# Loading the mixed weight block through GpSimd's DMA queue, and three planned landing times, in a tanh-gated product of matrices on Trainium2

## The chip, the cores and the metric

The kernel runs on one core of a Trainium2 chip. A core has a matrix engine (TensorE, PE in the profile, with its weight loads shown apart as PEld), three engines for elementwise work (VectorE or DVE, ScalarE or ACT, GpSimd or POOL), a queue engine that only issues transfers (SyncE or SP) and 16 DMA engines that move data between HBM and the core's memories. The metric is the device time of one launch in microseconds; lower is better.

## The reference

```python
def setup_inputs():
    batch, m, k, n = 16, 512, 1024, 768
    ...
def reference(x, w1, w2):
    y1 = np.matmul(x, w1)
    y2 = np.matmul(x, w2)
    return (np.tanh(y1) * y2).astype(np.float32)
```

x is 16 x 512 x 1024, w1 and w2 are 1024 x 768, all float32. Read as one matrix, x has 8192 rows, which are 64 row tiles of 128. Each output row tile is 128 x 768.

## The kernel before

**Blocks.** The kernel works in float16 with float32 sums. The two weight matrices are kept in one tile `wh`, cut into three column blocks of 512: block a is the first 512 columns of w1, block b the first 512 of w2, and block g (the mixed block) the last 256 columns of w1 beside the last 256 of w2. Along the contraction each block has eight slices of 128 rows, k = 0 to 7, in two halves of four (`KH` = 4). A slice of a block is named by both: a5 is slice 5 of block a; the two parts of a slice of g come from w1 (t = 0) and from w2 (t = 1).

**Head.** The first four row tiles (`HEAD` = 4) are multiplied plainly: for each row tile, each block and each slice, one matrix instruction of 512 columns (L420). This work is what TensorE does while the weights come in: block a first, then g, then b. The rows of these tiles are transposed on TensorE (L370), and so are those of row tiles 4, 5 and 6; the transposed rows are copied out of PSUM by ScalarE or VectorE (L356, L358).

**Triples.** The other 60 row tiles are worked in 20 triples. Three row tiles with two halves of the contraction and three column blocks would be 18 products of half a contraction each; a scheme with sums of operands does with 15 (`C_OPS`, names p0 to p14). Each product is four matrix instructions of 512 columns (L443). Its operands are blocks of x or sums of them, named by a bit mask: x1 and x2 are the two halves of a triple's first row tile, x4 and x8 of its second, x16 and x32 of its third. VectorE makes the ten sums of x for each triple (L411, for instance x3 = x1 + x2, x11 = x3 - x8, x15 = x11 - x4) and, once, the eleven sums of weight blocks (L402). ScalarE copies some results out of PSUM (L447), VectorE adds them up (L453), ScalarE takes the tanh (L456) and VectorE multiplies (L461). The order of the products is a fixed list; the first triple begins with p7 (x16 with a weight block), p10 (x32), p1 (x3), p6 (x15), p12, p9.

**The order of everything else** comes from a planner in the file (`Planner`). Each operation has a cost on each engine that may do it, a due time, and what it needs. The planner runs a simulated clock with these costs and writes out every engine's instructions in the order of its simulated starts. An engine then works through its list in that order on the chip: when an instruction at the head waits, all those behind it wait. How well the written order fits therefore depends on the planner's guesses, above all on when transfers land. Two kinds of guess are touched here:

- For the first loads there is a table `lands`. From a clock of 9.2 us on, each load in turn adds its size (`size`: 0.68 for half a row tile or a slice of a, 0.75 for a part of g, 0.63 for a slice of b, 1.25 for a row tile), and what would land after 21.5 us gets 1.2 us on top (`LAG_FROM`, `LAG`).
- A DMA transpose of a later row tile (operation T, issued by SP at L377) is planned to land its `latency` after its turn on the planner's one transfer line: 1.0 us for row tiles 7 to 9, and 3.0 us from row tile 10 on.

**Loads of the weights.** Slices a0 to a3 go out from ScalarE's queue and a4 to a7 from SP's (L347), as float32 into a staging area (`arena`), from which VectorE casts them into `wh` (L358). Block g follows on SP's queue in eight loads (L344); one load brings slices k and k + 4 of one of the two matrices, 128 partitions times two runs of 256 float32 numbers. When both matrices' parts have landed, slices k and k + 4 are cast into `wh`: slice 0 by VectorE (L358), the seven others by ScalarE (L356). Block b is loaded by GpSimd's queue in eight loads of one slice (L349), whose transfer itself turns float32 into float16, so that nothing is staged or cast. GpSimd is held back by a small instruction that reads a slice of `wh` (`gate`, L483): it begins its loads when slice g0 is cast. Behind block b on the same queue come the row tiles 6, 4 and 5 in this order (`rows_in`, L352, with the cast in the transfer too), and then all later row tiles. From row tile 10 on, each of these loads stands behind a second small instruction (`hold_loads`, L480) that waits for the transpose of the row tile four before.

Beside this, ScalarE sums the absolute values of every row tile and every weight slice (L380); at the end a flag is made of the sums, and only if they lie outside a range does a slower general path run.

Of the kernel before, what the change touches and what calls it, by code (L numbers as in the profile page):

```python
# [226 lines left out]
def kernel(  # L227
# [7 lines left out]
    nc = tc.nc  # L235
# [3 lines left out]
    KO = K // P  # L239
    KH = KO // 2  # L240
# [71 lines left out]
    def wf(s, k, n=1):  # L312
        j = slices.index((s, k)) % SLOTS
        return arena[:, j * F:(j + n) * F]
# [27 lines left out]
    def load_w(e, s, k, t=None):  # L342
        if s == "g":
            pin(nc.sync.dma_start(wf(s, k, 2).rearrange("p (h t n) -> p h t n", h=2, t=2)[:, :, t, :],  # L344
                                  wr[t].rearrange("p (h q) n -> p h q n", h=2)[:, :, k, F:]))
        elif s == "a":
            pin((nc.scalar if k < 4 else nc.sync).dma_start(wf(s, k), wr[0][:, k, :F]))  # L347
        else:
            pin(nc.gpsimd.dma_start(w_cols(s, k), wr[1][:, k, :F]))  # L349
# [170 lines left out]
    for n, what in enumerate(on_sp):  # L520
        before = [f"L{on_sp[n - 1]}"] if n else []
        if what[0] == "x":
            op(f"L{what}", {"sp": 0.05}, 0.1 * n - 100, [], load_first, int(what[1]), int(what[2]), issued=before, lands=lands[what])
        else:
            s, k = what[0], int(what[1])
            j = slices.index((s, k))
            old = [slices[i - SLOTS] for i in range(j, j + 1 + (s == "g")) if i >= SLOTS]
            op(f"L{what}", {"sp": 0.05}, 0.1 * n - 100, [], load_w, s, k, int(what[2]) if s == "g" else None, issued=before,
               behind=[f"c{a}{b}" for a, b in old], lands=lands[what])
    op("gate", {"pool": 0.1}, 0.0, ["c%s%d" % GATE], gate, *GATE)  # L530
    for n, what in enumerate(late):
        op(f"c{what}", {"pool": 0.58}, 0.1 * n, [], load_w, "b", int(what[1]), issued=[f"c{late[n - 1]}" if n else "gate"], lands=lands[what])
    for n, mt in enumerate(rows_in):
        op(f"L{mt}", {"pool": 0.58}, 1 + 0.1 * n, [], load_x, mt, issued=[f"L{rows_in[n - 1]}" if n else f"c{late[-1]}"],
           behind=[f"cx{m}{h}" for m in range(2, HEAD) for h in range(2) if xh_place(m) == xh_place(mt)], lands=lands[f"x{mt}"])

    landed = {}
    for s, k in slices:
        loads = [f"g{k % KH}{t}" for t in range(2)] if s == "g" else [f"{s}{k}"]
        landed[s, k] = max(lands[n] for n in loads)  # L540
        if s != "b":
            op(f"c{s}{k}", CAST.get(f"{s}{k}", CAST[s]), landed[s, k] + 0.3, [f"L{n}" for n in loads], cast_w, s, k)
    all_casts = [f"c{s}{k}" for s, k in slices if s != "b"]
    for t in range(2):
        for k in range(KO):
            late = START + 32 + 8 * (t * KO + k)
            op(f"aw{t}{k}", {"act": 0.81}, late + 6, [f"cg{k}", f"c{'ab'[t]}{k}"], abs_w, t, k, hold=late)

# [23 lines left out]
    def plain(mt, s, due, behind=()):  # L572
        for n, k in enumerate([k for u, k in slices if u == s]):
            before = list(behind) + ([f"m{mt}{s}0"] if n else [])
            op(f"m{mt}{s}{k}", {"pe": MM}, due(n), [f"c{s}{k}", f"e{mt}{k // KH}"], mm, (s, mt), mt, k, w_cols(s, k), n == 0,
               behind=before, chains=[(s, mt)])
        last = [f"m{mt}{s}{k}" for k in range(KO)]
        xt_readers[mt] += last
        return last
# [60 lines left out]
    def w_needs(v, ks=slice(0, KH)):  # L640
        if v in wsum:
            return [f"B{v}.{p.start}" for p in parts(v) if p.start < ks.stop and ks.start < p.stop]
        bit = v.bit_length() - 1
        return [f"c{s}{bit // 3 * KH + k}" for s in "abg"[bit % 3] for k in range(ks.start, ks.stop)]

# [81 lines left out]
    for mt in range(BY_PE, MT):  # L727
# [3 lines left out]
        if mt >= BY_PE + FREE:  # L731
# [133 lines left out]
```

## Time and profile before

| | |
|---|---|
| median of 3 runs | 298.4 us (298.35 to 298.59) |
| the profiled execution | 298.26 us, of which the profile's span is 296.7 us |
| TensorE busy | 289.9 us, 98% of the span, 1374 instructions |
| VectorE busy | 257.4 us, 87% |
| ScalarE busy | 225.9 us, 76% |
| GpSimd busy | 49.9 us, 17% |
| granted clock of TensorE | 0.999 |

TensorE is busy nearly all the time, so a microsecond can be won or lost only where it starts late, waits, or ends late. A busy share doesn't say whether its instructions follow each other at full pace, since the ends of matrix instructions are modelled; the distance from one start to the next does. A row of the timeline gives the start, the time taken, engine, line, operation, tiles written and read, and how many instructions are merged into it; in brackets stands the idle time ahead of it and what ended it. `arena` is the staging area for weights in the head and a buffer for partial results later; `early_x` is the first rows' buffer and later that of the sums of x.

### The profile page before, as it was taken

What the parts mean: (1) busy time and instruction counts of PE and PEld (TensorE: products, weight loads), DVE (VectorE), ACT (ScalarE), POOL (GpSimd) and SP (SyncE); (2) the same over time, 40 slices, a digit from 0 to 9 for tenths busy, and PEclk for the clock granted to TensorE, in tenths of its full rate; (3) what the DMA queues carried; (4) which work ended last, traced back from release to release, by engine and by line L of the source; (5) the groups of instructions that cost most, each with busy time, mean ns of one, the idle gap of its engine ahead of it and who ended that gap; (6) DMA issues with size and microseconds to landing.
All of it is one profiled execution on the core that took longest, in us unless ns stands there. A gap on an engine that the chain in (4) does not pass through costs nothing. (4 is left out here: it accounts for less than half of the span.)

```text
span 296.7 us, 4680 instructions
## 1 busy us (share of the span) xinstructions
PE 289.9 (98%) x1374; PEld 132.3 (45%) x1374; DVE 257.4 (87%) x552; ACT 225.9 (76%) x453; POOL 49.9 (17%) x129
## 2 busy tenths in 40 slices
PE   7999999999999999999999999999999999999994
PEld 3444444444444444444444444444444444444442
DVE  1679899989999998888989898898989989898784
ACT  2686898799978979797797988768687776868441
POOL 0073034032210321102111021111121100000000
PEclk9999999999999999999999999999999999999999
DMA  6999999999999999999999999999999999440334
GB/s 218 388 305 207 180 154 166 202 220 250 225 222 170 232 290 246 209 176 218 248 257 225 234 253 210 187 201 268 216 272 268 197 202 228 194 161 32 128 142 162
DMA packets 84427, 63.51 MB, mean 214 GB/s; under 512 B 62768, under 2 KB 66608, under 8 KB 84400
## 3 DMA queue, kind: packets, MB, share of 16 engines
q1 hardware_dynamic: 73600, 44.84, 63.2%
q0 software_dynamic: 9792, 16.78, 37.7%
q10 hardware_dynamic: 1008, 1.57, 1.5%
q8 instruction: 11, 0.18, 0.3%
q14 instruction: 16, 0.13, 0.1%
HBM read 39.85 MB, written 25.17 MB: 219 GB/s over the span
## 5 line engine op out<-in xcount | busy, mean ns | idle before, releaser
L443 PE MATMUL bank<-b,early_x 128*128 128x512 f16 x640 | 148.3, 379 | 0.1
L443 PEld LDWEIGHTS <-early_x 128*128 128x128 f16 x800 | 78.1, 98 | 95.0 <-issue 0.7
L453 DVE TENSOR_TENSOR bank<-bank,arena 128x512 f32<-128x512 f32 x100 | 69.7, 698 | 14.8 <-ACT arena L447 9.3
L447 ACT ACTIVATE arena<-bank 128x512 f32<-128x512 f32 x100 | 59.2, 596 | 28.4 <-PE bank L443 28.2
L461 DVE TENSOR_TENSOR o<-o,bank 128x256 f32<-128x256 f32 (+1 forms) x132 | 64.4, 513 | 6.1 <-ACT o L456 5.5
L380 ACT ACTIVATE junk<-xh 128x1024 f16<-128x1024 f16 x60 | 63.3, 1056 | 0.2
L443 PEld LDWEIGHTS <-xT 128*128 128x128 f16 x400 | 39.0, 98 | 47.2 <-issue 1.1
L443 PE MATMUL bank<-b,xT 128*128 128x512 f16 x240 | 58.3, 379 | 0.0
L456 ACT ACTIVATE o<-bank 128x256 f32<-128x256 f32 (+1 forms) x80 | 34.4, 436 | 16.8 <-DVE bank L453 12.9
L443 PE MATMUL bank<-wh,xT 128*128 128x512 f16 x160 | 41.1, 379 | 0.3 <-DVE bank L453 0.3
L443 PE MATMUL bank<-wh,early_x 128*128 128x512 f16 x160 | 40.9, 379 | 0.0
L480 POOL CAST held<-xT 128x1 f32<-128x1 f16 x54 | 13.0, 241 | 152.4 <-DMA xT<-xh 152.4
L352 POOL DMA_DIRECT2D xh<-in_x_dram x60 | 31.7, 529 | 23.3 <-ACT o L456 10.4
L411 DVE TENSOR_TENSOR early_x<-early_x,xT 128x512 f16<-128x512 f16 x80 | 33.3, 420 | 0.5
L447 ACT ACTIVATE bank<-bank 128x512 f32<-128x512 f32 x40 | 21.6, 575 | 7.6 <-DVE bank L453 6.4
L456 ACT ACTIVATE o<-arena 128x512 f32<-128x512 f32 x40 | 25.1, 628 | 1.3 <-DVE arena L453 1.1
L420 PE MATMUL bank<-wh,xT 128*128 128x512 f16 x72 | 18.6, 379 | 0.3 <-ACT xT L356 0.2
L411 DVE TENSOR_TENSOR early_x<-xT,xT 128x512 f16<-128x512 f16 x40 | 16.8, 421 | 0.0
L411 DVE TENSOR_TENSOR early_x<-xT,early_x 128x512 f16<-128x512 f16 x40 | 16.8, 420 | 0.0
L453 DVE TENSOR_TENSOR bank<-arena,bank 128x512 f32<-128x512 f32 x20 | 13.9, 695 | 2.3 <-ACT o L456 0.7
L453 DVE TENSOR_TENSOR arena<-bank,arena 128x512 f32<-128x512 f32 x20 | 13.7, 684 | 0.1
L453 DVE TENSOR_TENSOR arena<-arena,bank 128x512 f32<-128x512 f32 x20 | 13.6, 682 | 0.0
(47 smaller groups left out, 136.0 us busy)
## 6 DMA issues: line engine op xcount, KB each, us to landing
out_dram<-o SPq DMA_DIRECT2D x60, 384.0 KB, 5.6
xh<-in_x_dram POOLq DMA_DIRECT2D x60, 256.0 KB, 6.8
arena<-in_w_dram SPq DMA_DIRECT2D x12, 256.0 KB, 5.5
early_x<-in_x_dram SPq DMA_DIRECT2D x8, 256.0 KB, 5.0
arena<-in_w_dram ACTq DMA_DIRECT2D x4, 256.0 KB, 5.9
wh<-in_w_dram POOLq DMA_DIRECT2D x8, 128.0 KB, 5.4
xT<-xh SPq DMA_TRANSPOSE x57, 7.1
out_dram<-o SPq DMA_DIRECT2D x4, 128.0 KB, 2.2
```

The source lines that it names most:

```text
L352: pin(nc.gpsimd.dma_start(xh(mt), xf[mt]))
L380: pin(nc.scalar.activation(junk[:, :src.shape[-1]], src, ACT.Abs, scale=scale, accum_out=sums[:, column:column + 1]))
L411: pin(engine[e].tensor_tensor(x_operand(i, v), x_operand(i, a), x_operand(i, b), OP[how]))
L420: pin(nc.tensor.matmul(bank(chain)[:, :rhs.shape[-1]], xt(mt)[:, k, :], rhs, start=first, stop=k == KO - 1, skip_group_check=True))
L443: pin(nc.tensor.matmul(place(i, dst), x_operand(i, a)[:, k, :], w_rhs(b, k), start=begins and k == 0, stop=k == KH - 1, skip_group_check=T ...
L447: pin(nc.scalar.activation(place(i, dst), place(i, src), ACT.Copy, scale=float(sign)))
L453: pin(nc.vector.tensor_tensor(place(i, dst), a, b, ALU.add if signs == (1, 1) else ALU.subtract))
L456: pin(nc.scalar.activation(out_tile(HEAD + 3 * i + r)[:, lo:lo + n], place(i, src)[:, :n], ACT.Tanh, scale=float(sign)))
L461: pin(nc.vector.tensor_tensor(o, o, place(i, src)[:, at:at + n], ALU.mult))
L480: pin(nc.gpsimd.tensor_copy(held, xt(mt)[:, 0, :1]))
```

## The change

Three things are edited.

- Block g is no longer loaded by SP as float32 and cast afterwards. GpSimd's queue loads it with the cast in the transfer, straight into `wh`: eight loads as before, of slices k and k + 4 of one matrix, ahead of the eight loads of block b. The casts of g on VectorE (one) and ScalarE (seven) are gone, and so are the waits for their staging slots.
- GpSimd's gate waits for the cast of slice a5 in place of that of g0. In the table `lands`, a part of g adds 0.7 us in place of 0.75. A load of g has the same planned cost on GpSimd as one of b, 0.58 us.
- The planned latency of the transposes of row tiles 10, 11 and 12 becomes 5.8, 4.1 and 3.9 us in place of 3.0 (`LANDING`).

Since the planner runs anew with other numbers, the order of all engines' instructions may change with this, beyond the lines that are edited; the fixed order of the products doesn't.

```diff
+    LANDING = {HEAD + 6: 5.8, HEAD + 7: 4.1, HEAD + 8: 3.9}
...
         if s == "g":
-            pin(nc.sync.dma_start(wf(s, k, 2).rearrange("p (h t n) -> p h t n", h=2, t=2)[:, :, t, :],
-                                  wr[t].rearrange("p (h q) n -> p h q n", h=2)[:, :, k, F:]))
+            pin(nc.gpsimd.dma_start(wh[:, k::KH, F + t * G:F + t * G + G], wr[t][:, k::KH, F:]))
...
-    CAST = {"a": {"dve": 0.37}, "g": {"act": 0.495}, "g0": {"dve": 0.37}}
+    CAST = {"a": {"dve": 0.37}}
...
-    on_sp = "x00 x10 x20 x30 x01 x11 a4 a5 x21 a6 x31 a7".split() + [f"g{k}{t}" for k in range(KH) for t in range(2)]
-    late = [f"b{k}" for s, k in slices if s == "b"]
+    on_sp = "x00 x10 x20 x30 x01 x11 a4 a5 x21 a6 x31 a7".split()
+    late = [f"g{k}{t}" for k in range(KH) for t in range(2)] + [f"b{k}" for s, k in slices if s == "b"]
     rows_in = (HEAD + 2, HEAD, HEAD + 1)
-    GATE = ("g", 0)
+    GATE = ("a", 5)
     in_order = on_sp[4:] + late + [f"x{mt}" for mt in rows_in]
-    size = {"x": 0.68, "a": 0.68, "g": 0.75, "b": 0.63}
+    size = {"x": 0.68, "a": 0.68, "g": 0.7, "b": 0.63}
...
     for n, what in enumerate(late):
-        op(f"c{what}", {"pool": 0.58}, 0.1 * n, [], load_w, "b", int(what[1]), issued=[f"c{late[n - 1]}" if n else "gate"], lands=lands[what])
+        op(f"c{what}", {"pool": 0.58}, 0.1 * n, [], load_w, what[0], int(what[1]), int(what[2:] or 0), issued=[f"c{late[n - 1]}" if n else "gate"], lands=lands[what])
...
+    def cast(s, k):
+        return [f"cg{k % KH}{t}" for t in range(2)] if s == "g" else [f"c{s}{k}"]
...
-        loads = [f"g{k % KH}{t}" for t in range(2)] if s == "g" else [f"{s}{k}"]
-        landed[s, k] = max(lands[n] for n in loads)
-        if s != "b":
-            op(f"c{s}{k}", CAST.get(f"{s}{k}", CAST[s]), landed[s, k] + 0.3, [f"L{n}" for n in loads], cast_w, s, k)
+        landed[s, k] = max(lands[n[1:]] for n in cast(s, k))
+        if s == "a":
+            op(f"ca{k}", CAST["a"], landed[s, k] + 0.3, [f"La{k}"], cast_w, s, k)
...
-           behind=xt_readers[mt - XT_BUFS] if mt >= XT_BUFS and mt - XT_BUFS != HEAD - 1 else [], xfer=1.2, latency=1.0 if mt < HEAD + 6 else 3.0)
+           behind=xt_readers[mt - XT_BUFS] if mt >= XT_BUFS and mt - XT_BUFS != HEAD - 1 else [], xfer=1.2, latency=LANDING.get(mt, 1.0 if mt < HEAD + 6 else 3.0))
```

More of the change, by code (lines that the diff above doesn't have):

```diff
@@ L524 @@
         else:
[L525 to L529, printed above, removed]
+            op(f"L{what}", {"sp": 0.05}, 0.1 * n - 100, [], load_w, "a", int(what[1]), issued=before, lands=lands[what])
     op("gate", {"pool": 0.1}, 0.0, ["c%s%d" % GATE], gate, *GATE)
     for n, what in enumerate(late):
[L532 removed]
+        op(f"c{what}", {"pool": 0.58}, 0.1 * n, [], load_w, what[0], int(what[1]), int(what[2:] or 0), issued=[f"c{late[n - 1]}" if n else "gate"], lands=lands[what])
     for n, mt in enumerate(rows_in):
@@ L643, in w_needs @@
         bit = v.bit_length() - 1
-        return [f"c{s}{bit // 3 * KH + k}" for s in "abg"[bit % 3] for k in range(ks.start, ks.stop)]
+        return [n for k in range(ks.start, ks.stop) for n in cast("abg"[bit % 3], bit // 3 * KH + k)]
     for v, a, b, how in B_SUMS:
```

6 lines of the change are left out of this document (3 added, 3 removed).

## The prediction

> **What bounds the kernel now.** I read the busy table first, then stretches of time, then the rows around each stretch in which TensorE is short of full. The table by stretches (PE busy with its instruction count first, then PEld, DVE, ACT, POOL, granted clock, DMA share, GB/s):
>
> ```profile
> 15.00:28.00 13.00, 13.00 (x65) 5.91 (x63) 11.44 (x28) 10.82 (x22) 7.91 (x15) 1.00 1.16 260
> 28.00:36.00 8.00, 7.87 (x55) 3.95 (x53) 7.07 (x15) 6.20 (x12) 0.00 (x0) 1.00 1.10 174
> 48.00:53.00 5.00, 4.66 (x22) 1.99 (x21) 4.82 (x13) 3.92 (x10) 3.42 (x8) 1.00 1.10 187
> 120.00:200.00 80.00, 80.00 (x373) 36.25 (x371) 71.80 (x149) 65.06 (x134) 13.92 (x38) 1.00 1.18 223
> 200.00:280.00 80.00, 80.00 (x373) 36.27 (x372) 71.61 (x151) 58.73 (x116) 7.54 (x20) 1.00 0.89 200
> ```
>
> From 120 to 280 us TensorE has no hole, at full clock: 80 us for 373 matrix instructions is 0.215 us each. The change can therefore win only in the first 60 us, and whatever it loses there moves the whole rest. The ends of matrix instructions are modelled, so a hole is read from starts, and shows smaller in the busy column. Two holes of some size are left there. The rows around them, in time order (start, time taken, engine, line, tiles):
>
> ```profile
> 31.99 2.20 PE L443 MATMUL bank<-b,early_x 128*128 128x512 f16 x8
> 33.15 0.76 PEld L443 LDWEIGHTS <-early_x 128*128 128x128 f16 x5 [0.63 <-DVE early_x L411]
> 49.73 1.89 PE L443 MATMUL bank<-b,early_x 128*128 128x512 f16 x8
> 51.96 1.02 PE L443 MATMUL bank<-wh,xT 128*128 128x512 f16 x4 [0.34 <-DVE bank L453]
> ```
>
> The first: p1 starts at 31.99 and has four instructions, so p6 could start at 32.85; its weight load starts at 33.15, after a sum of x on VectorE. That is 0.30 us. The second: eight instructions from 49.73 end at 51.45, the next starts at 51.96 after a VectorE addition. That is 0.51 us.
>
> Where does the first hole come from? Product p6 needs x15, a sum that takes in row tile 5. Its load is the last of three on GpSimd's queue behind block b. The queue's rows, and then the answers for the loads issued at 17.2 to 21.0 (block b), at 21.48 (row tile 6) and at 23.99 (row tile 5), which give the time to landing (of block b the durations of the issues too, in ns):
>
> ```profile
> 16.81 0.44 POOL L483 CAST held<-wh 128x1 f32<-128x1 f16 x1 [15.27 <-DVE wh L358]
> 17.19 4.37 POOL L349 DMA_DIRECT2D wh<-in_w_dram  x8
> 21.48 1.26 POOL L352 DMA_DIRECT2D xh<-in_x_dram  x2
> 23.99 0.53 POOL L352 DMA_DIRECT2D xh<-in_x_dram  x1 [1.24 <-DMA wh<-in_w_dram]
> ```
> ```profile
> L349 POOL DMA_DIRECT2D wh<-in_w_dram x8: 535/571/667, 17.2 to 21.0; - x8
> ...
> DMA to landing us min/median/max: 4.0/5.4/5.9
> ```
> ```profile
> xh<-in_x_dram POOLq DMA_DIRECT2D x1, 256.0 KB, 6.6
> ```
>
> The last row is the answer for 21.48 and, with the same number, for 23.99: row tile 6 lands at 28.1 and row tile 5 at 30.6. Two row tiles in 2.5 us are 1.25 us each: the DMA engines are busy (share 1.10 and 1.16 above) and a load lands when those ahead have gone through. TensorE's transposes of the second, and VectorE's sums:
>
> ```profile
> 30.68 0.61 PE L370 MATMUL bank<-ident_h,xh 128*128 128x128 f16 x8
> ```
> ```profile
> 31.80 1.30 DVE L411 TENSOR_TENSOR early_x<-early_x,xT 128x512 f16<-128x512 f16 x3
> ```
>
> Row tile 5 is transposed at 30.68, right at its landing, and p6 follows 2.55 us after that landing (33.15 less 30.6) through transposes, copies and sums. So the start of p6 is either TensorE's own backlog (32.85) or the landing of row tile 5 plus 2.55, whichever is later. That is what the first part of the change moves.
>
> **The change, part by part.**
>
> *Casts removed.* ScalarE and VectorE lose these:
>
> ```profile
> L356 ACT CAST wh<-arena 128x512 f16<-128x512 f32 x7 | 4.0, 615 | 0.3 <-DMA arena<-in_w_dram 0.3
> ```
> ```profile
> 12.01 0.43 DVE L358 CAST wh<-arena 128x512 f16<-128x512 f32 x1 [0.24 <-DMA arena<-in_w_dram]
> 12.69 0.43 DVE L358 CAST xh<-early_x 128x512 f16<-128x512 f32 x1 [0.26 <-DMA early_x<-in_x_dram]
> 13.37 0.43 DVE L358 CAST wh<-arena 128x512 f16<-128x512 f32 x1 [0.25 <-DMA arena<-in_w_dram]
> 14.05 0.43 DVE L358 CAST xh<-early_x 128x512 f16<-128x512 f32 x1 [0.25 <-DMA early_x<-in_x_dram]
> 14.74 0.43 DVE L358 CAST wh<-arena 128x512 f16<-128x512 f32 x1 [0.26 <-DMA arena<-in_w_dram]
> 16.32 0.43 DVE L358 CAST wh<-arena 128x512 f16<-128x512 f32 x1 [1.15 <-DMA arena<-in_w_dram]
> ```
>
> That is 4.0 us of ScalarE and 0.43 us of VectorE (the row at 16.32). Worth on the path: nothing, since TensorE is full from 15 to 28 us and neither cast is in the chain of p6. SP loses eight issues that nothing waits behind until its first transpose.
>
> *The loads of g on GpSimd's queue.* The gate opens when a5 is cast, 12.44 (the row at 12.01 plus 0.43). Today the first load is issued 0.44 us after the cast that opens it (16.75 to 17.19), so g's first goes out at 12.88. When does it land? The rows of today's g on SP's queue, the last load of block a ahead of it (issued 9.82), and the nearest load that starts on an idle GpSimd queue, at 36.85, with the microseconds after it:
>
> ```profile
> L344 SPq DMA_DIRECT2D arena<-in_w_dram x8: 367/368/467, 10.3 to 14.7; - x8
> ...
> DMA to landing us min/median/max: 5.2/5.8/6.0
> ```
> ```profile
> arena<-in_w_dram SPq DMA_DIRECT2D x1, 256.0 KB, 4.9
> ```
> ```profile
> 36.85 0.53 POOL L352 DMA_DIRECT2D xh<-in_x_dram  x1
> ```
> ```profile
> xh<-in_x_dram POOLq DMA_DIRECT2D x1, 256.0 KB, 4.0
> ```
> ```profile
> 38.00:39.00 1.00, 1.00 (x7) 0.43 (x5) 1.00 (x3) 1.00 (x3) 1.00 (x3) 1.00 0.62 41
> 39.00:40.00 1.00, 1.00 (x6) 0.43 (x5) 1.00 (x3) 1.00 (x4) 0.37 (x3) 1.00 0.92 172
> ```
>
> Block a is in at 14.7. Today g follows it without a pause and its eight loads come in every 0.75 us, the first at 10.29 + 5.2 = 15.5 and the last at 14.73 + 6.0 = 20.7 (least and greatest time to landing). A load on the idle GpSimd queue lands 4.0 us after its issue, of which 1.25 is its own transfer; in the second before 39 us the engines move 41 GB/s, in the next 172. So 2.75 us pass beside the transfer. For the transfer itself the packets of GpSimd's queue from 20 to 21 us (packets, MB, share) bear on it:
>
> ```profile
> q0 software_dynamic: 210, 0.20, 120.7%
> ```
>
> They are block b's, 128 to a load, so 0.61 us for the same bytes. On SP's queue g takes 0.75 in runs of the same length. I price a g load's transfer at 0.72, near the second. The first then lands at 12.88 + 2.75 + 0.72 = 16.35, and the DMA engines have stood idle for 0.9 us: bounds 0 (block b took over from SP's queue with the DMA share at 1.16 throughout, issued 3.5 us ahead of that queue's last landing, 17.19 against 20.7) and 0.9 (the row at 36.85). I take 0.9, the nearer: 12.88 is only 1.8 us ahead of 14.7.
>
> *Issue time.* A load of b or of x costs GpSimd 0.53 us (4.37 us for eight overlapping; 0.53 at 36.85), with 128 runs of 2 or 4 KB. One of g has 256 runs of 1 KB. Bytes don't count; whether runs do no row shows. Bounds: 0.53 and 1.06. I take 0.80. The eighth load is then issued at 12.88 + 7 x 0.80 = 18.48 and lands 3.47 later, at 21.95, against 16.35 + 7 x 0.72 = 21.4 if transfers set the pace. The Trainium skill, "DMA: Bandwidth & Descriptors", section "Anatomy of one DMA", says of descriptor generation "small, variable" and that many can be emitted before a cost shows; by that rule the pace would be the transfers' and the result 0.55 us less than mine. The equal 0.53 us for 2 and 4 KB runs neither bears it out nor speaks against it.
>
> *Sum for the first part.* g's last part lands at 21.95 in place of 20.7: +1.2 us. Everything behind it on the queue (b, row tiles 6, 4, 5) keeps its distance. The ninth load waits for the landing of the first, as row tile 5 does today for one of b (1.24 us above); that landing, 16.35, is before its turn at 19.3, so this costs nothing. TensorE itself needs the first pair of g at about 16.84 (the gate's row stands there, with g0 cast) and gets it at 17.15, 0.3 us late; it uses 1.72 us for a pair (eight instructions) while pairs come every 1.6, so that is the only delay, and it is inside the 1.2, because p6 takes the later of the two. Row tile 5 lands at 31.8, p6 starts at 34.35: +1.2 us. Bounds: the plan's table says 0.4 us earlier than today, which can only be used to TensorE's backlog: -0.3. The other end, issue of 1.06, puts g's last part at 12.88 + 7.42 + 3.47 = 23.8: +3.1.
>
> *The planned landings.* The second hole: VectorE's list has sums for row tile 10 before the addition that TensorE waits for.
>
> ```profile
> 48.18 0.43 DVE L411 TENSOR_TENSOR early_x<-xT 128x512 f16<-128x512 f16 x1 [0.25 <-DMA xT<-xh]
> ...
> 51.12 0.69 DVE L453 TENSOR_TENSOR bank<-arena,bank 128x512 f32<-128x512 f32 x1
> ```
> ```profile
> xT<-xh SPq DMA_TRANSPOSE x1, 7.3
> ```
>
> The transpose of row tile 10 is issued at 40.9 and lands 7.3 later, at 48.2; VectorE waits 0.25 us for it and comes to the addition at 51.12. With a planned latency 2.8 us longer these sums move behind work that is ready, and the addition comes forward by more than the hole. I take -0.5; bounds -0.5 and 0 (another order puts another late item there). If row tiles 7 to 9 and so the transposes come 1.2 us later, TensorE does too, and the hole neither grows nor shrinks by it.
>
> *The sum.* +1.2 - 0.5 = +0.7 on the profiled execution's 298.26, 298.96; the median of the runs is 0.14 above it: 299.1 us. A move under 0.2% (0.6 us) I call none, since that is about what a measurement of this kernel can tell from no change.
>
> **Rivals.**
>
> *Faster: the loads land as the new table has it.* No idle time, issue at 0.53, so row tile 5 lands 0.4 us earlier and both holes close: -0.3 - 0.5 gives 297.6. For it speaks that today's table fits today's landings (14.6 planned for a7, 14.7 measured); against it the 4.0 us from an idle queue.
>
> *No change: transfers set the pace.* Idle time 0.9, issue under 0.72: g's last part at 21.4, +0.7 - 0.5: 298.6.
>
> *Slower: VectorE's casts keep GpSimd from writing its descriptors.* From 12.7 to 15.2 four casts follow with 0.25 us between them. If GpSimd can prepare a load only in these gaps, the first (0.53 us) takes two gaps and a bit, done at 14.5 in place of 13.4, and the second ends at 15.5: 1.3 us on top, so +2.5 - 0.5: 300.4. It decides from one cast's hold (0.43 us) on. Today no load is issued beside such casts; b's, beside sums of two inputs, took 0.54 to 0.67. The Trainium skill, "SBUF — State Buffer", section "SBUF: two separate sides", has this rule: a float32 copy on VectorE locks GpSimd out of a shared port, and descriptors wait. Today's trace has no row for or against it.
>
> *Much slower: issue by runs, 1.06 us:* +3.1 - 0.5 gives 301.0.
>
> **How the numbers follow.** My forecast 0.28 (own range 298.9 to 299.6), landing as planned 0.20, no change 0.27, casts in the way 0.14, issue by runs 0.11. Faster is the second alone, 0.20; same the third, 0.27; slower the rest, 0.53. The range, 297.6 to 300.5, leaves out the last case and some of the fastest.
>
> **What would show it.** GpSimd's first load at 12.9 and eight of g by their own durations (0.53, 0.8, 1.06); first pair of g landed at 17.1; a DMA share under 1 near 15 us; row tile 5 landed near 31.8 and p6's wait there; no hole at 51.5. Wrong makes it an issue of 0.53 with no idle time, or a new hole after 36 us from the new order.

## The result, and the profile after

| | before | after |
|---|---|---|
| median of the runs | 298.31 us (297.85 to 298.59, six runs) | 302.72 us (300.9 to 314.96, six runs) |
| ratio | | 1.014, 95% interval 1.0119 to 1.0161 |
| the profiled execution | 298.26 us, span 296.7 | 300.90 us, span 299.4 |
| a second set of runs | 298.38 us | 301.12 us (300.79 to 302.06), ratio 1.0096, interval 1.0068 to 1.0125 |

The change makes the kernel slower, by 1.4% in the first set of runs and 1.0% in the second. The runs of the changed kernel lie further apart than those of the kernel before (the longest, 314.96 us, at a mean granted clock of 0.989, but one of 303.12 us at 1.000), and why stays open; what follows explains the profiled execution, 2.64 us longer than that of before, whose clock was 0.998.

The busy time of the page first, then the table by stretches, for the stretches that the prediction showed of the kernel before (PE with its count, PEld, DVE, ACT, POOL, granted clock, DMA share, GB/s):

```profile
PE 290.3 (97%) x1374; PEld 131.6 (44%) x1374; DVE 255.5 (85%) x551; ACT 222.4 (74%) x446; POOL 55.6 (19%) x137
```
```profile
15.00:28.00 13.00, 12.51 (x61) 5.33 (x60) 9.66 (x24) 7.30 (x15) 10.66 (x19) 1.00 1.20 170
28.00:36.00 8.00, 6.89 (x50) 3.36 (x48) 7.25 (x15) 5.11 (x10) 0.62 (x2) 1.00 1.10 197
48.00:53.00 5.00, 4.93 (x24) 2.15 (x23) 4.97 (x12) 4.75 (x10) 1.93 (x6) 1.00 1.22 171
120.00:200.00 80.00, 80.00 (x373) 36.24 (x372) 70.42 (x148) 66.51 (x136) 14.85 (x38) 1.00 1.18 226
200.00:280.00 80.00, 80.00 (x373) 36.28 (x372) 71.74 (x153) 57.19 (x114) 8.32 (x22) 1.00 1.00 198
```

From 120 to 280 us nothing is different for TensorE. It was full from 15 to 28 us before, and now has holes there and more behind them. The timeline of the weight loads, in brackets the idle time of PEld and what ended it, shows what TensorE waits for:

```profile
17.02 0.80 PEld L420 LDWEIGHTS <-xT 128*128 128x128 f16 x5 [0.28 <-DMA wh<-in_w_dram]
...
19.43 0.98 PEld L420 LDWEIGHTS <-xT 128*128 128x128 f16 x6 [0.97 <-DMA wh<-in_w_dram]
...
21.35 0.98 PEld L420 LDWEIGHTS <-xT 128*128 128x128 f16 x6 [0.51 <-DMA wh<-in_w_dram]
...
30.27 0.45 PEld L370 LDWEIGHTS <-xh 128*128 128x128 f16 x8 [1.47 <-DMA xh<-in_x_dram]
...
31.53 0.45 PEld L370 LDWEIGHTS <-xh 128*128 128x128 f16 x8 [0.49 <-DMA xh<-in_x_dram]
...
35.53 1.41 PEld L443 LDWEIGHTS <-early_x 128*128 128x128 f16 x8 [0.63 <-DVE early_x L411]
```

Three waits for parts of g, then the loads of row tiles 6 (30.27) and 4 (31.53), and p6 at 35.53, 2.38 us later than before (33.15). The rows of GpSimd's queue, and what the answers for the first load of g and for the last two say of issue and landing:

```profile
12.85 0.18 POOL L483 CAST held<-wh 128x1 f32<-128x1 f16 x1 [11.31 <-DVE wh L358]
12.97 5.83 POOL L345 DMA_DIRECT2D wh<-in_w_dram  x8
18.80 3.32 POOL L349 DMA_DIRECT2D wh<-in_w_dram  x6
```
```profile
L345 POOL DMA_DIRECT2D wh<-in_w_dram x1: 839/839/839, 13.0 to 13.0; - x1
...
DMA to landing us min/median/max: 3.2/3.2/3.2
```
```profile
L345 POOL DMA_DIRECT2D wh<-in_w_dram x2: 716/716/716, 17.4 to 18.1; - x2
...
DMA to landing us min/median/max: 4.7/4.7/4.7
```

The first part of g lands at 16.2 and the last at 22.8 (18.1 plus 4.7), which before was 20.7. The issues are not the reason: at 0.716 us each they end at 18.8. The table in steps of one microsecond shows the transfer itself (last column GB/s, ahead of it the share of the DMA engines):

```profile
13.00:14.00 1.00, 1.00 (x8) 0.52 (x8) 0.72 (x2) 0.94 (x2) 1.00 (x3) 1.00 1.00 369
14.00:15.00 1.00, 0.81 (x5) 0.30 (x4) 0.57 (x2) 0.59 (x1) 1.00 (x2) 1.00 0.57 63
15.00:16.00 1.00, 1.00 (x10) 0.52 (x8) 0.48 (x1) 0.46 (x1) 1.00 (x3) 1.00 1.17 153
16.00:17.00 1.00, 1.00 (x6) 0.32 (x4) 0.00 (x0) 1.00 (x4) 1.00 (x2) 1.00 1.27 165
17.00:18.00 1.00, 1.00 (x7) 0.51 (x6) 0.86 (x3) 1.00 (x4) 1.00 (x2) 1.00 1.01 102
18.00:19.00 1.00, 0.96 (x5) 0.23 (x3) 0.75 (x2) 1.00 (x3) 1.00 (x3) 1.00 0.98 124
19.00:20.00 1.00, 0.56 (x3) 0.31 (x4) 0.52 (x2) 0.97 (x3) 1.00 (x3) 1.00 1.25 163
```

There is a thin stretch from 14 to 15 us, where I had foreseen idle engines. They aren't idle: the first packet of GpSimd's queue starts at 14.52, just as the last of SP's queue ends (14.54), but several of the first packets take 0.4 to 0.5 us each. And there is a second fall from 17 to 19 us that I had not foreseen: 102 and 124 GB/s where 165 had been reached. In these two microseconds single packets of 512 bytes take 0.4 to 0.9 us where the others take about 0.06. The third part of g lands 1.57 us after the second (18.55 against 16.98).

The 2.64 us, with starts and landings from the two traces:

| from, to | before | after | difference |
|---|---|---|---|
| last load of block a lands | 14.71 | 14.99 | +0.28 |
| from there to the last part of g | 6.01 | 7.78 | +1.77 |
| from there to row tile 5 | 9.89 | 10.02 | +0.13 |
| from there to the start of p6 | 2.54 | 2.75 | +0.21 |
| from p6 to TensorE's last start (holes of 0.50 at 51.2 and 0.13 at 65.6 before; 0.23 at 49.3 after) | 259.03 | 258.63 | -0.40 |
| from there to the end of the span | 4.54 | 5.19 | +0.65 |

The last line is the one that I had not looked at. The last store takes 2.25 us to land before and 2.58 after; then a wait of SP's among its last ones, for signals long given, takes 0.37 us in place of 0.06.

The landings hold something else that the prediction didn't see, in both kernels. The landing of a load is sixteen signals in the trace, as many as there are DMA engines; call them its parts. In the kernel before fifteen parts of row tile 5 are in at 29.42 us and the last one at 30.61; in the changed kernel at 32.06 and 32.79, and of row tile 6, which TensorE waits for, at 29.59 and 30.22. Such a lag begins near a fetch of 16 KB of instructions that takes 0.96 us (at 21.50 before, 23.02 after) and stays with every load behind: in the kernel before the last part of the second load of b comes 0.17 us after the fifteenth, that of the third 1.29 us. That the fetch holds up one DMA engine fits in time and size, but no run here tested it. As both kernels have it, and the changed one the smaller lag, it isn't what makes that one slower.

### The profile page after: what moved, and what is told of

It is laid out like the page before. It is cut to its first block, busy times and chain, and to the rows that moved or that the text cites. A ratio compares the mean times of both kernels' runs of the same rounds, so it can differ in the third digit from the quotient of the medians.

```text
span 299.4 us, 4655 instructions
## 1 busy us (share of the span) xinstructions
PE 290.3 (97%) x1374; PEld 131.6 (44%) x1374; DVE 255.5 (85%) x551; ACT 222.4 (74%) x446; POOL 55.6 (19%) x137
## 3 DMA queue, kind: packets, MB, share of 16 engines
q10 hardware_dynamic: 1008, 1.57, 1.5%
## 5 line engine op out<-in xcount | busy, mean ns | idle before, releaser
L352 POOL DMA_DIRECT2D xh<-in_x_dram x60 | 31.9, 531 | 21.3 <-ACT o L456 8.3
```

The costliest lines, as they stand in the source:

```text
L352: pin(nc.gpsimd.dma_start(xh(mt), xf[mt]))
```

## Experiments

**The two parts apart.** One kernel is the one before with the planned landings alone, another the changed kernel without them.

```diff
+    LANDING = {HEAD + 6: 5.8, HEAD + 7: 4.1, HEAD + 8: 3.9}
-... latency=1.0 if mt < HEAD + 6 else 3.0)
+... latency=LANDING.get(mt, 1.0 if mt < HEAD + 6 else 3.0))
```

> The kernel before with the three planned landings alone; block g stays on SP's queue with its casts. Theory A (the late queue makes the loss, the planned landings help): the hole at 51.5 us goes, the first 40 us stay, 297.8 us, 0.3 to 0.5 less than before. Theory B (the new order of the planner is what hurts): 299 us or more, with holes that before didn't have.

> The kernel before with the planned landings of the transposes of row tiles 10 to 12 and nothing else, a second time in more rounds. The first time it ran at 0.998 of the kernel before with an interval that holds 1; the hole at 51.2 us shrank from 0.50 to 0.28 us. Theory 'this part is worth what its hole lost, 0.2 to 0.3 us': ratio 0.999, time 0.2 to 0.3 us under the kernel before. My prediction's term: -0.5, 0.9983. Rival 'no gain': ratio 1.0000 or more.

Measured: 297.88 us both times, against 298.38 and 298.28 of the kernel before; ratios 0.998 (0.9954 to 1.0006) and 0.9987 (0.9973 to 1.0001), so by the times alone a gain is likely and not shown. The traces show it: from p6 to TensorE's last start it takes 258.67 us in both profiles, 0.36 less than before: the hole ahead of the product at 51.5 shrank from 0.50 to 0.28 and 0.14 us but did not go, and a hole of 0.13 us at 65.6 went, which I had not listed. The rows of the first of the two (eight instructions from 49.94 end at 51.67 by 0.216 us each; VectorE's addition now starts at 50.78 and not at 51.12):

```profile
49.94 1.89 PE L444 MATMUL bank<-b,early_x 128*128 128x512 f16 x8
51.94 1.02 PE L444 MATMUL bank<-wh,xT 128*128 128x512 f16 x4
```
```profile
50.45 0.42 DVE L412 TENSOR_TENSOR early_x<-early_x,xT 128x512 f16<-128x512 f16 x1
50.78 0.69 DVE L454 TENSOR_TENSOR bank<-arena,bank 128x512 f32<-128x512 f32 x1
```

The other one:

```diff
-    LANDING = {HEAD + 6: 5.8, HEAD + 7: 4.1, HEAD + 8: 3.9}
+    LANDING = {}
```

> The changed kernel without the three planned landings; block g on GpSimd's queue. Theory A: row tile 5 lands near 32.8 us and p6 starts near 35.5 as in the changed kernel, and the hole near 51.5 is back at 0.5: as slow as the changed kernel or up to 0.4 us slower. Theory B: nearer to before than the changed kernel is, under 300 us.

Measured: 300.61 us (300.27 to 302.52), ratio 1.0077 (1.005 to 1.0103). The loss is the loads' alone. From p6 to TensorE's last start it takes 258.62 us here too, without the planned landings: once p6 comes 2 us later, the two holes close by themselves. Beside the first part the second is worth nothing that can be seen.

**Is it the written order, or the transfer?** The plan has g landing from 15.5 on without a break; if the engines' lists were bad because of that, a table with the traced landings would mend them. The changed kernel was run beside it again.

```diff
+    lands.update(zip(late, (16.2, 17.0, 18.6, 19.4, 20.6, 21.3, 22.1, 22.8, 23.8, 25.2, 25.8, 26.4, 27.0, 27.7, 28.4, 29.0)))
+    lands.update(zip([f"x{mt}" for mt in rows_in], (30.2, 31.5, 32.8)))
```

> The changed kernel with the table of first landings set to what its trace shows (g 16.2 to 22.8, b 23.8 to 29.0, row tiles 6, 4 and 5 at 30.2, 31.5 and 32.8), so that the written order fits them. Theory A: p6 still follows the landing of row tile 5 by 2.55 us, so within 0.4 us of the changed kernel. Theory C (the loss is that engines stand in line behind items planned too early): 1 to 2 us faster than the changed kernel.

> The changed kernel once more, for its spread: its runs lie between 300.9 and 304.9 us where those of before lie within 0.7. Theory A: the time goes with the landing of row tile 5, which moves from run to run, since the loads of g pause for a varying time near 17 us. Theory D: the landings are the same in each run and the granted clock of TensorE drops for some microseconds after the waits near 19 and 29 us, as means of 0.990 in the longest runs hint.

Measured: 302.69 us (four runs, 301.80 to 321.05), ratio 1.0123 (1.0072 to 1.0174), against 301.12 for the changed kernel. The table with the true landings mends nothing: row tile 5 lands at 32.89, much as in the changed kernel, and TensorE now waits 1.12 us for a sum at 34.0 and 0.47 us for another at 36.5, so that its last start is 0.71 us later. The other 1.13 us by which this span is longer lie in the tail (6.32 us; see below). This order is not better, and with the row tile landing at 32.89 no order could start p6 where it started before (33.15), since transposes, copies and sums stand between (2.47 us with the gate at a3, below). The landings cost the 2 us.

The changed kernel's second trace has the last part of g at 22.52 and row tile 5 at 33.02, 0.23 us later than in the first, and its span is 0.22 us longer, at a granted clock of 1.000. Between these two executions the time goes with the landing, as theory A has it; theory D wasn't tested, since no long execution was traced.

**Is it the lead?** In the changed kernel the first load of g is issued 2.0 us ahead of the last landing on the queues before it (12.97 and 14.99); in the kernel before the first load of b had 3.5 us (17.19 and 20.72), and showed neither a thin stretch nor a long packet. Three edits change this lead and nothing else: every engine has the same instructions in the same order as without the edit. Two of them change the gate of the changed kernel, one to a3,

```diff
-    GATE = ("a", 5)
+    GATE = ("a", 3)
```

and the other to a4 in the same line:

> The changed kernel with its gate two casts earlier: GpSimd's first load waits for the cast of a3 (ends 10.34 us in the second profile of the changed kernel) and not for that of a5 (12.64), so it is issued near 10.5 in place of 12.82 and every load of g is written 2.3 us earlier. Theory 'the queue runs dry': the pauses of g's transfer (packets of 0.4 to 1.4 us between 16.4 and 18.8, third load 1.3 to 2.3 us after the second) come because the DMA engines stand close behind GpSimd's descriptor writing. With the lead the pauses go: third load within 0.9 us of the second, no packet over 0.35 us between 16 and 19 us, last part of g near 20.9 in place of 22.5, row tile 5 near 31.4, p6 near 34.1, time about 299.6 (1.4 to 1.7 us under the changed kernel). What it costs: from 13 to 15 us a6, the last quarter of x and a7 share the DMA engines with g and land up to 1.3 us later; TensorE then waits there and not for g. Rival 'casting packets of 512 bytes pause whatever the lead': a third load 1.3 us or more after the second, packets of 0.4 us and more between 16 and 19 us, pitch 0.94, last part of g at 21.3 or later, time 300.2 or more. Rival 'the earlier loads take from a': a7 later than 16.2 and time 301 or more.

> The changed kernel with its gate one cast earlier: the cast of a4 ends at 11.97 in the second profile of the changed kernel, so the first load of g is issued near 12.15, 0.67 us earlier. Theory 'the queue runs dry': the first packets reach the DMA engines near 14.6, as block a ends, so the slow start between 14.2 and 15.0 goes; the pause after the second load remains in part, since the lead of 0.67 us is eaten by the third load. Last part of g 21.3 to 21.9, time 300.1 to 300.5. Rival 'pauses whatever the lead': everything of g moves by 0.67 and no more, pauses as long as before, last part of g at 21.85, 300.45. Rival 'the earlier loads take from a': a7 later by 0.7 or more and time not under that of the changed kernel.

The third is made in the kernel before, for block b:

```diff
-    GATE = ("g", 0)
+    GATE = ("g", 1)
```

> The kernel before with its gate later: GpSimd's first load of block b waits for the cast of g1 (ends near 18.4 us) and not for that of g0 (16.75), so it is issued near 18.8, some 2 us ahead of SP's last landing (20.7), as in the changed kernel GpSimd's first load is issued 2 us ahead of the end of block a. Theory 'a small lead makes the transfer slow, whatever is loaded': an empty stretch of up to 0.8 us, then packets of 0.35 us and more between 21 and 25 us (none in the kernel before but one instruction fetch) and landings of b unevenly spaced; last b 28.0 or later in place of 26.8, p6 34.3 or later in place of 33.16, time 299.4 or more. Rival 'the pauses belong to the 512-byte packets of g': the empty stretch alone, then b every 0.62 us without long packets, last b near 27.5, time 298.9 to 299.1.

Measured (the lead is from the first issue on GpSimd's queue to the last landing ahead; packets are those of that queue from the first issue to the eighth landing, without those of 4 bytes, and long ones are over 0.35 us):

| kernel | loads | lead | packets, of them long | longest | from the last landing ahead to the eighth load's | time, ratio |
|---|---|---|---|---|---|---|
| before | b | 3.5 us | 1192, 0 | 0.19 us | 6.1 us | 298.3 |
| late_b | b | 1.9 us | 1121, 28 | 0.78 us | 7.3 us | 300.4, 1.0082 (1.0067 to 1.0096) |
| after | g | 2.0 us | 2187, 24 | 0.89 us | 7.8 us | 302.7, 1.014 |
| after_again | g | 2.0 us | 2204, 15 | 1.03 us | 7.7 us | 301.1, 1.0096 |
| gate_a4 | g | 2.7 us | 2281, 11 | 1.18 us | 7.8 us | 300.15, 1.0072 (1.0046 to 1.0099) |
| gate_a3 | g | 4.3 us | 2188, 0 | 0.10 us | 5.3 us | 298.38, 1.0011 (0.9996 to 1.0027) |

With a lead of 3.5 us and more there is no long packet, with 2.7 and less there are, whichever block is loaded and whether its packets have 512 or 1024 bytes. (The kernel with g alone and the one with the traced landings, both with a lead of 2.0 us, have 27 and 25 long ones.) A single landing misleads here: in the kernel before, too, the third load of b lands 1.77 us after the second, but by its one late part; the other fifteen parts follow in 0.65 us. The steps of one microsecond with the gate at a3:

```profile
14.00:15.00 1.00, 1.00 (x6) 0.38 (x6) 0.58 (x2) 0.40 (x1) 1.00 (x3) 1.00 1.40 203
...
17.00:18.00 1.00, 1.00 (x7) 0.47 (x5) 0.97 (x3) 1.00 (x3) 1.00 (x3) 1.00 1.44 192
18.00:19.00 1.00, 1.00 (x6) 0.42 (x5) 0.93 (x4) 0.97 (x3) 1.00 (x4) 1.00 1.45 194
```

and for block b in the kernel with the later gate, where before there were 212, 209, 195 and 201 GB/s from 20 to 24 us:

```profile
20.00:21.00 1.00, 1.00 (x6) 0.47 (x5) 0.98 (x3) 0.67 (x3) 1.00 (x3) 1.00 0.77 100
21.00:22.00 1.00, 1.00 (x7) 0.45 (x5) 0.93 (x4) 1.00 (x3) 1.00 (x3) 1.00 1.12 174
22.00:23.00 1.00, 1.00 (x6) 0.43 (x5) 0.97 (x4) 1.00 (x3) 1.00 (x3) 1.00 1.00 118
23.00:24.00 1.00, 1.00 (x6) 0.49 (x5) 0.96 (x4) 1.00 (x5) 1.00 (x3) 1.00 0.97 126
```

The same picture as with g: a thin stretch, a rise, a second fall. Here p6 starts at 34.50, and TensorE's last start is 1.10 us later than before. With the gate at a4 I had expected the lead, longer by 0.67 us, to take away the slow start and part of the fall; the start was better, the pause stayed (third part 1.48 us after the second), and the last part of g landed at 22.48 and not at 21.3 to 21.9. The time still fell as expected, by another way: no part lags there (the last two of row tile 5 land at 31.52 and 31.59), and row tile 5 follows the last part of g by 9.1 us where it was 10.0. That g takes from block a when it starts earlier was not borne out: a7 lands at 14.82 with the gate at a3.

The gate at a3 also decides on another of my rivals, VectorE's casts. It puts the issue of g beside the casts of a4 to a7; GpSimd's rows there and the answer for its eight loads:

```profile
10.51 5.88 POOL L345 DMA_DIRECT2D wh<-in_w_dram  x8
```
```profile
L345 POOL DMA_DIRECT2D wh<-in_w_dram x8: 728/750/847, 10.5 to 15.6; - x8
...
DMA to landing us min/median/max: 4.5/4.6/4.8
```

The growth from 0.728 to 0.768 us isn't the casts' either: the changed kernel's second trace has the same growth with the later gate, and in the repeat of this kernel (below) the last six issues take 0.716 us each beside the same casts. Nothing is left of the rival's 1.3 us.

**What does a late row tile cost?** The kernel before, with row tile 5 loaded one time more ahead of row tile 6.

```diff
+        if mt == HEAD + 2:
+            pin(nc.gpsimd.dma_start(xh(HEAD + 5), xf[HEAD + 5]))
```

> The kernel before with one more load and nothing else: row tile 5 is loaded one time more, into its own buffer, on GpSimd's queue ahead of row tile 6, so row tiles 6, 4 and 5 land 1.25 us later and g and b stay where they are. Theory 'the start of p6 is the landing of row tile 5 plus 2.55 to 2.75 us, and what p6 loses the end loses': p6 starts at 34.4 to 34.6 in place of 33.16 and the time is 1.25 to 1.45 over the kernel before, 299.6 to 299.8. Rival 'TensorE takes part of it back in later holes' (0.50 at 51.2): 299.1 or less. Rival 'the three row tiles cost more than their own delay', since TensorE then has nothing to do ahead of row tile 6 too: 300.2 or more.

Measured: 299.44 us, ratio 1.0035 (1.0023 to 1.0047): 1.16 us. Row tile 5 lands at 31.82 in place of 30.61 (+1.21), and TensorE:

```profile
29.32 0.45 PEld L372 LDWEIGHTS <-xh 128*128 128x128 f16 x8 [1.15 <-DMA xh<-in_x_dram]
...
30.63 0.45 PEld L372 LDWEIGHTS <-xh 128*128 128x128 f16 x8 [0.75 <-DMA xh<-in_x_dram]
...
34.42 1.63 PEld L445 LDWEIGHTS <-early_x 128*128 128x128 f16 x9 [0.62 <-DVE early_x L413]
```

p6 is 1.27 us later, and 1.06 us of it are left at TensorE's last start (the hole at 51.2 is smaller). For p6 the landing costs one for one. It gains nothing the other way: with the gate at a3 row tile 5 lands at 29.95, 0.66 us earlier than in the kernel before, and the rows of its transposes and of p6 read

```profile
30.48 0.65 PEld L370 LDWEIGHTS <-xh 128*128 128x128 f16 x8
...
33.16 1.62 PEld L443 LDWEIGHTS <-early_x 128*128 128x128 f16 x9 [0.63 <-DVE early_x L411]
```

so p6 starts as before. The transposes of row tile 5 stand behind p7 in TensorE's list, and their first matrix instruction starts at 30.69 here and at 30.68 in the kernel before: there the row tile landed just in time by chance. The hole of 0.30 us ahead of p6 is there in all three kernels, whenever the row tile lands, so it isn't the landing's.

**Where does the tail come from?** With the gate at a3 TensorE's last start is at 291.56, 0.62 us ahead of the kernel before, and the span is 0.1 us longer. A repeat in more rounds:

> The changed kernel with the gate at a3 a second time, in more rounds. The first time 298.38 at a ratio of 1.0011 with an interval that holds 1. Its profiled execution has TensorE's last instruction 0.62 us earlier than the kernel before, and the span no shorter. Expected 298.3 to 298.5, ratio 1.000 to 1.001. If the tail were chance and the 0.62 us counted: 297.7, ratio 0.998.

Measured: 298.70 us, ratio 1.003 (1.0011 to 1.0049), a little more than expected; the profiled execution 298.29 with the last start at 291.48. So the early last start isn't worth anything, and the tail is no chance. The last store of the kernel before, and that with the gate at a3:

```profile
L417 SPq DMA_DIRECT2D out_dram<-o x2: 332/332/332, 292.7 to 293.4; - x2
...
DMA to landing us min/median/max: 2.1/2.2/2.3
```
```profile
L417 SPq DMA_DIRECT2D out_dram<-o x1: 333/333/333, 292.8 to 292.8; - x1
...
DMA to landing us min/median/max: 2.6/2.6/2.6
```

A store lands in sixteen parts too. With the gate at a3 fifteen land from 294.78 to 294.95 and the last at 295.36, behind a packet of 8 KB of instructions that starts at 294.75. The instructions that are left out and added change the length of each engine's program (in the trace, waits and branches among them, SP has 297 for 307, ScalarE 603 for 609, VectorE 705 for 724), and so where its code is fetched. Five kernels make programs longer again with work whose result nobody reads; all have the gate at a3 but the second, which is the changed kernel.

```diff
+            if k == KO - 1:
+                for n in range(8):
+                    pin(nc.sync.dma_start(spare[:, 16 * n:16 * n + 16], wr[0][:1, k, 16 * n:16 * n + 16]))
```

> The same with eight loads of 64 bytes on SP behind a7, into a tile that nobody reads, so that SP's program has as many instructions as that of the kernel before. In every profile with g on GpSimd's queue one of the sixteen parts of the last store lands about 0.4 us after the fifteen others, right behind a fetch of instructions of 8 KB, and the program ends 4.7 to 5.2 us after TensorE's last start in place of 4.5. Theory 'SP's shorter program moves a fetch of instructions onto the last store': the late part and SP's pause are gone, the tail is 4.5 again, time 297.7 to 297.9 (0.5 to 0.65 under the one without). Rival 'the fetch belongs to another engine, or to the order of stores': the tail stays, 298.3 or more.

> The changed kernel itself with the same eight small loads on SP. Theory as for the gate at a3: the tail is 4.5 us in place of 5.2, time 300.3 to 300.6 where the changed kernel had 301.1. Rival: the tail stays, 300.9 or more.

and on top of it, beside the sums of absolute values, six copies on ScalarE, nineteen on VectorE, or both (the lines that make the spare tiles are left out):

```diff
+        n = t * KO + k
+        if n < 6:
+            pin(nc.scalar.copy(spare_c[:, n:n + 1], ident[:, :1]))
+        for j in range(8 + n, 8 + n + 1) if n < 13 else range(8 + 13 + 2 * (n - 13), 8 + 15 + 2 * (n - 13)):
+            pin(nc.vector.tensor_copy(spare_c[:, j:j + 1], ident[:, :1]))
```

> The gate at a3 with the eight small loads on SP, and six copies of 128x1 on ScalarE beside the work on the absolute values (near 60 us), so that ScalarE's program too is as long as in the kernel before. One of sixteen parts of the last store still lands 0.4 us after the others, right behind a fetch of instructions of 8 KB that the longer SP program did not move. Theory 'it is ScalarE's fetch': the sixteen parts land within 0.25 us of one another, the last store 2.25 us after its issue in place of 2.6, tail 4.5 us. Rival 'VectorE's, or another's': the late part stays, tail 4.8 us.

> The gate at a3 with the eight small loads on SP, and nineteen copies of 128x1 on VectorE at the same places, so that VectorE's program is as long as in the kernel before (it has 19 instructions less in the changed one, waits and branches among them). Theory 'it is VectorE's fetch': late part gone, last store 2.25 us after its issue, tail 4.5 us. Rival 'ScalarE's, or another's': the late part stays, tail 4.8 us. The nineteen copies themselves (about 0.06 us each) lie beside TensorE's work and cost nothing.

> All three: SP, ScalarE and VectorE as long as in the kernel before, gate at a3. Theory 'the tail of the changed kernel is a matter of where the fetches of instructions fall': tail 4.5 us behind TensorE's last start as in the kernel before, and TensorE's last start 0.6 us earlier than there: 297.6 to 297.8, ratio 0.998, faster than the kernel before. Rival 'the tail belongs to something else that the changed order brings': 298.1 or more.

Measured:

| kernel | last of sixteen parts behind the fifteenth | TensorE's last start to the end of the span | time, ratio |
|---|---|---|---|
| before | 0.01 us | 4.54 us | 298.3 |
| after | 0.39 us | 5.19 us | 302.7 and 301.1 |
| g_only | 0.43 us | 4.94 us | 300.61, 1.0077 |
| traced_lands | 1.56 us | 6.32 us | 302.69, 1.0123 |
| gate_a3 | 0.41 us | 5.20 us | 298.38, 1.0011 |
| gate_a3_pad8 (SP) | 0.41 us | 4.88 us | 298.16, 1.0022 (0.9995 to 1.005) |
| after_pad8 (SP) | 0.41 us | 4.88 us | 304.47, 1.0137 (1.0086 to 1.0188); the profiled execution 315.54 at a mean granted clock of 0.98 |
| pad_act (SP, ScalarE) | 0.44 us | 4.92 us | one run, 298.49 |
| pad_dve (SP, VectorE) | 0.01 us | 4.55 us | one run, 310.39 at a mean granted clock of 0.98 |
| pad_all (SP, ScalarE, VectorE) | 0.01 us | 4.52 us | 297.89, 0.9986 (0.9973 to 0.9998) |

The tail has two halves. SP's pause goes with SP's length (5.20 to 4.88): it is in every trace in which SP's program has 297 instructions, and in none with 298 (g_only), 305 (with the small loads, two short of the kernel before) or more. The late part of the last store goes with VectorE's length and not with ScalarE's (4.92 against 4.55). With the nineteen copies (0.14 to 0.15 us each, not 0.06) the fetch ahead of it, of 0.31 us, is gone too:

```profile
q14 instruction: 2, 0.02, 1.0%
```
```profile
q14 instruction: 1, 0.01, 0.7%
```

The first row is of pad_act, the second of pad_dve, each for the last 4 to 5 us. This fetch and the late part come together in all nine traces in which VectorE's program has 704 or 705 instructions, and neither is there with 721 or 724; so the fetch is most likely VectorE's. The fetch that is left (0.52 us at 295.14 in the kernel before) makes no part late. In traced_lands, with 742 instructions on VectorE, one of 16 KB and 0.94 us starts at 297.00, and the last part comes 1.56 us behind the others. Of pad_dve and after_pad8 only the tail is read.

With the lead and the tail mended, the edit is 0.14% faster than the kernel before (0.3 us of medians), with an interval that ends just under 1. That lies between the theory (297.6 to 297.8) and its rival (298.1), and is no better than the planned landings alone (297.88). In the trace p6 starts at 33.37, not earlier than before, and TensorE's last start is 0.39 us earlier, not 0.6; the two holes at 51.2 and 65.6 are what is gained. g on GpSimd's queue gains nothing that TensorE could use.

## Why the prediction was wrong

The sign and the place were right, the size was not: 298.96 us for a profiled execution of 300.90. Of the 1.94 us in between, 0.54 are the transfer of g, 0.28 the later landing of block a in that execution, 0.36 the way from g to p6, 0.11 the planned landings, and 0.65 the tail, which the sum doesn't have. The median of the first set of runs, 302.72, lies another 1.8 us higher, which no trace explains. By its own steps:

- *Casts removed, worth nothing.* Right: TensorE had waited for none of them.
- *First load at 12.88; 0.9 us of idle DMA engines; first landing at 16.35.* Right in the first and the last (12.97 and 16.17), the last by luck: the engines weren't idle for 0.9 us, packets ran from 14.52 on, and the first load's took 1.65 us in place of 0.72. The price of 0.72 itself was near: with enough lead the parts of g come in every 0.68 us. (Of the 210 packets that I divided by 128, 16 have 4 bytes; without them it is 0.66 us a load and not 0.61.)
- *Issue 0.80 us.* Measured 0.716 for 256 runs against 0.53 for 128, between my bounds. The rule that I took from the Trainium skill ("DMA: Bandwidth & Descriptors", "Anatomy of one DMA"), that descriptor generation is small, is not borne out in this trace: 0.19 us more for 128 more runs. It isn't what sets the pace, though: the eight issues end at 18.8 and the last part lands at 22.8.
- *The last part of g at the eighth issue plus 3.47.* This is the step that failed, and the term of the sum that was too small. I took the time from issue to landing as fixed once the queue runs. It was 3.2 us for the first two loads, 4.0 for the third and 4.7 for the last, since the transfer pauses when the DMA engines stand close behind GpSimd's issue. From the last landing of block a it took 7.78 us and not 7.24, and 5.3 when the lead was 4.3 us. The row of the idle queue at 36.85, from which I took the price, was a single load: it showed the slow start and could not show the second fall. The kernel before had the other end of it in view, a lead of 3.5 us without a pause, and I used it only as a bound.
- *p6 is the landing of row tile 5 plus 2.55, everything behind g keeps its distance.* Nearly: 2.75 and 0.13 us more on the way. But the 2.55 counts from the transposes, which stand behind p7 in TensorE's list, and not from the landing, as the gate at a3 shows; so my "faster" rival could not have won its 0.3 us. TensorE was late at row tile 6 already (30.27), which I had not followed. And the queue ahead doesn't set the landing of these row tiles alone, as I had read it: one late part adds 1.19 us to that of row tile 5 before and 0.73 after.
- *Planned landings, -0.5.* -0.36 alone in the trace, -0.4 to -0.5 in the medians (with intervals that hold 1); the hole did not go, and part of the gain came from another at 65.6. Beside the first part it is worth nothing, since a later p6 closes the holes by itself: the two terms of the sum could not be added.
- *Nothing behind TensorE's last instruction.* +0.65 us, a step that the prediction doesn't have. I had counted the instructions that go and come by their time, not by where the code behind them would be fetched.

Against the rivals: *casts in the way* gave 300.4, near the measured time, and is refuted as a mechanism by the issues beside the casts with the gate at a3, 0.72 to 0.77 us, of which the repeat leaves 0.716. The Trainium skill's rule ("SBUF — State Buffer", "SBUF: two separate sides") doesn't show here, where the copies are casts to float16: the first issue takes 0.84 to 0.85 us in every kernel with g on this queue, and the others take no longer beside casts than elsewhere. *Issue by runs, 1.06* gave 301.0, nearer still, by luck: it is refuted by 0.716. *Landing as planned* and *transfers set the pace* fail with the pause; the second is what the gate at a3 makes true.

## What to carry to other kernels

When loads move to GpSimd's queue behind another queue, look at the lead: issue the first of them well ahead of the last landing on the queue before (here 3.5 us did and 2.7 did not), and read the GB/s of each microsecond, since issue times and single landings can hide a pause or feign one. A landing that TensorE's backlog covers gains nothing when it comes earlier and costs nearly one for one when it comes later (1.06 us of 1.21 here), so give such loads room rather than a tight plan. When an edit moves instructions between engines, compare the tail too, from the last matrix instruction to the end.

## What was not expected of the hardware

- Packets of GpSimd's queue that take 0.4 to 1.4 us in place of 0.06 to 0.1, mostly in bursts near the start of the transfer, if the lead is small: 11 to 28 of some 2200 (or 1100) in six traces with leads of 1.9 to 2.7 us, and none over 0.19 us in the two kernels with 3.5 and 4.3 us (one of 0.43 us in that with eight small loads on SP). That the lead decides is shown; why is not. What the DMA engine does in that time the records don't show. That the descriptors (the orders that GpSimd writes for the DMA engines) aren't ready was only argued, and the issue of the third load ends at 15.2 us, 1.7 us ahead of the second landing.
- An issue on GpSimd depends on the runs and not on the bytes: 0.53 us for 128 runs of 2 or 4 KB, 0.716 for 256 runs of 1 KB.
- One fetch of 8 KB of instructions behind TensorE's last instruction goes with a last store that lands 0.33 to 0.4 us later, since one of its sixteen parts comes late. Nineteen more instructions on VectorE took both away. In traced_lands one of 16 KB goes with a tail of 6.32 us. The Trainium skill ("Runtime: NRT & Kernel Launch", "Instruction fetch mechanics") says that crossing a block of instructions is mostly hidden. At the end of the program these runs show otherwise, and in its middle the late parts of the row tiles speak against it: TensorE waits for row tile 6 until 30.22 us, when fifteen of its sixteen parts have been in since 29.59.
